# A hybrid decoder step on one core: three logit banks, probabilities in five tiles, and another order for marking and for the opening

## The chip, the cores and the metric

The kernel runs on one core of one Trainium2 chip. The metric is the time of one execution in microseconds (us) on the device, taken as the median of three runs. A profile of one execution (the trace) is read beside it. TensorE is PE in the profile and its weight loads are PEld; VectorE is DVE, ScalarE is ACT, GpSimd is POOL, and SyncE (SP) issues most of the DMA transfers.

## The reference, cut to what matters

One inference step of a decoder layer: a prompt of 1024 tokens and 8 sequences of 4 sampled tokens with 1024 cached keys each, width 1024, all in float32. The input is normalised and modulated by a condition, multiplied by one wide matrix, and split into an attention part, an indexer part, a retention part and gates.

```python
h, gate = modulated_input(x, c, w_ada, b_ada, g_norm)          # silu(c) @ w_ada: shift, scale, gate
qa, ka, va, za, qi, ki, wi, qr, kr, vr, zr, ga, gr = split_projection(h @ w_in)
s = sum_h relu(qi_h @ ki.T) * wi_h                             # index scores, 4 heads of 64
idx = top_k(where(key <= query, s, -inf), 256)                 # exact top 256, ties by lower index
y_a = softmax(qa @ k[idx] / 8) @ v[idx] * silu(za)             # 8 heads of 64
y_r = group_norm(retention(rotary(qr), rotary(kr), vr)) * g_ret * silu(zr)
merged = sigmoid(ga) * (y_a @ w_pa) + sigmoid(gr) * (y_r @ w_pr)
y = rms_norm(x + gate * (merged @ w_out), g_final)
```

It also returns the new keys, values, indexer keys and retention states.

## The kernel before, in words

Precision comes from splitting: a float32 operand becomes a rounded high part and a low rest, and a product is three matmuls (high by high, high by low, low by high). Rounding is a copy on ScalarE, the rest a subtraction on VectorE or GpSimd. The stages, by the profile's time:

1. **Opening (0 to 63 us).** `x_load` fetches the tokens, `x_block` turns them, `norms` finds their scales. For each of eight slices k of the width, `load_wa(k)` fetches two blocks of 512 KB of `w_ada`, `modulation(k)` multiplies them by the conditions (L212), turns the sums (L328) and reduces them to `cm`; `h_tile(k)` makes the modulated input `HH[k]` and its rest `HL[k]` (ScalarE L348, VectorE L349). `start_two(W)` (L235) begins the first two projections as the slices appear; its weights `ws` are loaded after `load_wa(0)`, rounded at L395 and L398 and their rests taken at L400. `idle_products` are matmuls of zeros, which fill PE.
2. **Projections, index scores, search, retention (63 to 545 us).** `project_parts` runs the projections (L218 to L220) from the list `order`. In their shadow VectorE and ScalarE search the 256th largest score of every query bit by bit (`pick_all`, `count`, `count_signs`); `exact` and `finish` then mark the keys that are not picked. `finish(j)` counts (L870), compares for equality on GpSimd (L922), numbers the equal ones by a scan (L923), combines (L924, L925) and writes the mask `BI[b]` in bf16 on ScalarE (L926). Its index j is 0 to 4 for blocks 6 to 2, 5 (`NP - 2`) for block 7, and 6 (`NP - 1`) for the sampled tokens. `retention` works pair by pair of heads; `gate_rows` makes a part of the output gate by products (L212), a copy (L523), a sum over partitions (L525) and a store.
3. **Cached keys and values (545 to 810 us).** Projections go on while GpSimd gathers cache pages (L1061, with the row numbers `idx` from L1051) for the sampled tokens.
4. **Prompt attention (810 to 967 us).** Sixteen steps (four pairs of heads, each in four pairs of query blocks that make nine key blocks together). `logits` multiplies (L1214, L1215) into a bank `lg`, VectorE adds the mask and takes the maximum (L1216), ScalarE the exponential, GpSimd the scale (L1223). `turn` transposes the probabilities by PE into a bank `tr` (L1236) and copies them to the tile `PT` (L1238); `combine` multiplies them by the values into a bank `po` (L1253, 36 products), and every second step VectorE reads `po` out (L1259). Logits run two steps ahead. `side` is the retention part's output projection (L1024 to L1026), in pieces of 12 matmuls, put between the steps.
5. **Output (967 to 1115 us).** The attention's and the final projection, the norm, the stores.

PSUM has eight banks in the attention: `lg` 2, `tr` 2, `po` 2, and `pj` 2 for the projections.

Each engine executes its own queue in order. The order of each queue is written before the run by a planner, which simulates the program with its own costs and takes the instruction that it finds ready, by priority (the order of the source). `issue_after(x)` makes the instructions inside it follow x on x's engine. Tiles are handed out by name from pools with a number of buffers: a writer waits until the readers of the buffer's last content are done.

Of the kernel before, what the change touches and what calls it, by code (L numbers as in the profile page):

```python
# [8 lines left out]
F32 = mybir.dt.float32  # L9
F32R = mybir.dt.float32r  # L10
BF = mybir.dt.bfloat16
# [106 lines left out]
def _hybrid_step(ctx, tc, A, outs, dbg):  # L118
# [122 lines left out]
    with ExitStack() as s0:  # L241
# [92 lines left out]
        def h_tile(k, pm):  # L334

            shift = BB[:, k, 0:1]
            nc.scalar.activation(AA[:, k], pm[:, 9:18], AF.Identity, bias=cg[:, k:k + 1], scale=cols[:, 24 + k:25 + k])
            nc.scalar.activation(shift, pm[:, 0:1], AF.Identity, bias=cols[:, k:k + 1])
            h = XT[:, k]
            nc.vector.scalar_tensor_tensor(h[:, :T], h[:, :T], AA[:, k, 0:1], RB[:, :T], op0=OP.mult, op1=OP.mult)  # L340
# [28 lines left out]
        W, ws = [], []  # L369
        zeros = sp.tile([128, 640], BF, name="zeros")  # L370
        nc.vector.memset(zeros, 0.0)

        def idle_products(n, behind):

            x = pl()
            with tc.issue_after(behind):
                for i in range(n):
                    nc.tensor.matmul(x[:, 512 * (i % 2):512 * (i % 2) + 512], zeros[:, :128], zeros[:, 128:], start=True, stop=True)

        for k in range(KT):  # L380
            load_wa(k)
            if k == 0:
                with tc.issue_after(loads[-1].ins):
                    ws = [wload(wp, w_in, f, 128) for f in (O_KI, O_QI)]
                pm, turned = modulation(k)
                idle_products(8, turned)
            else:
                with tc.issue_after(spread):
                    pm, turned = modulation(k)
            head_ends = h_tile(k, pm)  # L390
            if k == 0:
                for i in (0, 1):
                    wh, wl = [sp.tile([128, KT, 128], F32R, name="w", bufs=4) for _ in "hl"]
                    if i == 0:
                        nc.scalar.copy(wh, ws[i])  # L395
                    else:
                        with tc.issue_after(head_ends[0].ins):
                            nc.scalar.copy(wh, ws[i])  # L398
                    with tc.issue_after(head_ends[1].ins):
                        nc.vector.tensor_sub(wl, ws[i], f32(wh))  # L400
                    W.append((wh, wl))
        first = start_two(W)
# [95 lines left out]
    def retention(gp):  # L498
        with ExitStack() as s3:
            rp = s3.enter_context(tc.tile_pool(name="rp", bufs=1, reuse_waits="tile"))  # L500
            RC = rp.tile([128, R_ALL], F32, name="rc")
            nc.sync.dma_start(RC, A["rcs"])
            O = rp.tile([128, 9, 2, 64], F32, name="O")
            nc.gpsimd.memset(O[:, 8], 0.0)
            SD = rp.tile([128, 8, 128], F32, name="SD")
            nc.gpsimd.memset(SD, 0.0)
            for p in range(4):
                rows = split_rows(gp, O_QA + 128 * p, p, q_rows, qs)
                pair(rp, RC, O, SD, p, rows)
                for _ in rows:  # L510
                    pass
                gates(gp, (4 + 2 * p,))
                gate_rows(rp, p)
                gates(gp, (5 + 2 * p,))

    def gate_rows(rp, p):

        x = pj()
        for o in (0, 1):
            w = wload(wp, A["w_ada"][0], 2 * D + 256 * p + 128 * o, 128)  # L520
            ada_rows(x[:, 128 * o:128 * o + 128], lambda k: w[:, k])
        parts_, sums = [rp.tile([128, CH], F32, name="zt", bufs=2)[:, :256] for _ in (0, 1)]
        nc.scalar.copy(parts_, x[:, :256])  # L523
        x = pj()
        nc.tensor.matmul(x[:32, :256], C[:, C_SEL:C_SEL + 32], parts_, start=True, stop=True)  # L525
        nc.scalar.copy(sums[:9], x[:9, :256])
        nc.scalar.dma_start(GD[:, 256 * p:256 * p + 256], sums[:9])

# [186 lines left out]


    k_out, v_out, ki_out, st_out, ks_out, vs_out, kis_out, sts_out = outs[2:]

    with ExitStack() as s1:
# [4 lines left out]
        with ExitStack() as s2:  # L724
# [74 lines left out]
            gidx = selp.tile([128, NB], I32, name="gidx")  # L799
            gio = ip.tile([128, NB], I32, name="gio")  # L800
# [113 lines left out]
        def finish(j):  # L914
# [6 lines left out]
            t = thr[:n, j:j + 1]  # L921
            nc.gpsimd.tensor_scalar(eq[:n, :W], sc, t, 1.0, op0=OP.is_equal, op1=OP.mult)  # L922
            nc.vector.tensor_tensor_scan(ra[:n, :W], eq[:n, :W], eq[:n, :W], 0.0, op0=OP.add, op1=OP.bypass)  # L923
            nc.vector.scalar_tensor_tensor(ra[:n, :W], ra[:n, :W], rem[:n, j:j + 1], eq[:n, :W], op0=OP.is_gt, op1=OP.mult)  # L924
            nc.vector.scalar_tensor_tensor(ra[:n, :W], sc, t, ra[:n, :W], op0=OP.is_lt, op1=OP.add)  # L925
            nc.scalar.activation(bi, ra[:n, :W], AF.Copy, scale=MASKNEG)  # L926

# [8 lines left out]
        def pick_all():  # L936
# [100 lines left out]

    QU = 2
    NQ = 8 // QU
    sv = ctx.enter_context(tc.tile_pool(name="sv", bufs=1, reuse_waits="tile"))  # L1040
# [7 lines left out]
    by_pair = lambda d: d[:, T:].rearrange("(h p) c -> p h c", p=128)  # L1048
    idx = sv.tile([128, NQ, NB], I32, name="idx")
    for u in range(NQ):  # L1050
        nc.vector.tensor_scalar(idx[:, u], gidx, float(NQ), float(u), op0=OP.mult, op1=OP.add)  # L1051
    ks, zs, YS = [sv.tile([128, 4, NS], F32, name=n) for n in ("ks", "zs", "ys")]
# [147 lines left out]
    def logits(ap, step):  # L1200
# [4 lines left out]
        for b in blocks:  # L1205
            W = (b + 1) * 128
            for i, (k, qh, ql) in enumerate(ops):
# [3 lines left out]
                for n0 in range(0, W, 512):  # L1211
                    n1 = min(W, n0 + 512)
                    x = pbank("lg", 2)
                    nc.tensor.matmul(x[:, :n1 - n0], qh[:, qb], k[:, n0:n1], start=True, stop=False)  # L1214
                    nc.tensor.matmul(x[:, :n1 - n0], ql[:, qb], k[:, n0:n1], start=False, stop=True)  # L1215
# [12 lines left out]
    def turn(ap, step):  # L1228

        lg = step["lg"]  # L1230
        PT = step["PT"] = ap.tile([128, 18, 128], F32, name="pT", bufs=1)
        for j0 in range(0, 18, 4):
# [4 lines left out]
            flip[0] += 1  # L1237
            (nc.vector.tensor_copy if flip[0] % 3 == 0 else nc.scalar.copy)(PT[:, j0:j0 + m].rearrange("p j c -> p (j c)"), x[:, :128 * m])  # L1238

    def combine(ap, step):  # L1240
# [3 lines left out]
        if step["half"] == 0:  # L1244
            step["po"][0] = pbank("po", 2)
        po = step["po"][0]

        slot = {b: i for i, b in enumerate(sorted(step["group"]))}
        run = [(b1, kb, b0 + 1 + kb) for kb in range(b1, -1, -1)] + [(b0, kb, kb) for kb in range(b0, -1, -1)]

        def product(b, kb, j, i):
            r = slice(64 * i, 64 * i + 64)
            return nc.tensor.matmul(po[r, 128 * slot[b]:128 * slot[b] + 128], V[:, kb, r], PT[:, 2 * j + i], start=(kb == b), stop=(kb == 0))  # L1253
        step["last"] = together([lambda b=b, kb=kb, j=j, i=i: product(b, kb, j, i) for b, kb, j in run for i in (1, 0)])
# [10 lines left out]
    with ExitStack() as s4:  # L1265
# [238 lines left out]
```

## Time and profile before

| what | value |
|---|---|
| median of three runs | 1117.72 us (1115.03 to 1120.34) |
| profiled execution, its own time | 1117.12 us |
| its span | 1115.3 us, 20512 instructions |
| busy, of the span | PE 97%, PEld 89%, DVE 61%, ACT 43%, POOL 23% |
| mean granted TensorE clock | 0.993 |
| DMA | 185.63 MB, 166 GB/s |

The list of waits tells for each engine which instruction stood still and who released it; the timeline lists the instructions with the idle time before them in brackets; a row of windows gives busy time by engine in a stretch. Matmul ends are modelled, so a PE that is shown busy can still wait a little.

### The profile page before, as it was taken

The page shows a single profiled execution, that of the slowest core. Times are in us where ns is not written, and L with a number is a line of the kernel's source. Part 1 is how long each engine was busy: PE and PEld are TensorE (multiplying, and loading weights), DVE is VectorE, ACT ScalarE, POOL GpSimd, SP SyncE. Part 2 cuts the span into 40 slices and gives each one's busy share as a digit, 9 for nine tenths or more (in the row PEclk, how much of TensorE's full clock was granted, in tenths as well). Part 3 has the DMA queues.
Part 4 walks back from the last instruction along what each step waited for, and adds up shares of the span by engine and source line. Part 5 has one row for each costly group of instructions (what it writes and reads, how often), then busy time and mean ns, then how long its engine had stood idle before and what let it go on. Part 6 is the DMA issues. An engine that isn't in the chain of part 4 may idle for free. (4 is left out here: it accounts for less than half of the span.)

```text
span 1115.3 us, 20512 instructions
## 1 busy us (share of the span) xinstructions
PE 1085.7 (97%) x8137; PEld 987.9 (89%) x8138; DVE 680.3 (61%) x1632; ACT 478.0 (43%) x923; POOL 253.4 (23%) x202
## 2 busy tenths in 40 slices
PE   7999999999999999989999999999999999999997
PEld 6889899899989989989999998887988888898776
DVE  6776349698877868888422222210356777497765
ACT  6574445554654455333343333311335666443211
POOL 0003006113311220263242222244113333100000
PEclk9999999999999999999999999999999999999999
DMA  9923335265244515523787757386797520367431
GB/s 308 243 72 105 112 101 151 54 203 140 82 149 126 164 46 181 155 61 92 256 286 232 234 183 247 112 286 240 243 310 273 182 99 30 111 202 257 152 122 58
DMA packets 156024, 185.63 MB, mean 166 GB/s; under 512 B 18630, under 2 KB 126990, under 8 KB 154839
## 3 DMA queue, kind: packets, MB, share of 16 engines
q1 hardware_dynamic: 145632, 147.80, 42.5%
q0 software_dynamic: 9856, 35.66, 9.5%
q8 instruction: 64, 1.05, 0.4%
q10 hardware_dynamic: 438, 0.86, 0.2%
q14 instruction: 34, 0.27, 0.1%
HBM read 139.33 MB, written 41.17 MB: 162 GB/s over the span
## 5 line engine op out<-in xcount | busy, mean ns | idle before, releaser
L218 PE MATMUL pj<-hh,wh 128*128 128x352 f32 (+1 forms) x1168 | 383.4, 328 | 0.3 <-DVE qs L747 0.3
L219 PE MATMUL pj<-hl,wh 128*128 128x352 f32 (+1 forms) x1168 | 379.6, 325 | 0.0
L220 PE MATMUL pj<-hh,wl 128*128 128x352 f32 (+1 forms) x1168 | 378.6, 324 | 0.0
L218 PEld LDWEIGHTS pj<-hh,wh 128*128 128x128 f32 x1168 | 219.8, 188 | 8.2 <-issue 6.7
L219 PEld LDWEIGHTS pj<-hl,wh 128*128 128x128 f32 x1168 | 220.5, 189 | 5.1 <-issue 4.6
L220 PEld LDWEIGHTS pj<-hh,wl 128*128 128x128 f32 x1168 | 219.9, 188 | 4.4 <-issue 4.0
L870 DVE TENSOR_SCALAR_CACHE_REDUCE eq<-sc,cand 128x896 bf16<-128x896 f32 (+4 forms) x155 | 135.7, 876 | 2.6
L204 ACT CAST wh<-ws 128x1024 fp32r<-128x1024 f32 (+1 forms) x65 | 61.0, 942 | 115.4 <-PE pj L219 79.1
L205 POOL TENSOR_TENSOR wl<-ws,wh 128x1024 fp32r<-128x1024 f32 x18 | 45.1, 2506 | 147.0 <-ACT wh L204 146.9
L1223 POOL TENSOR_SCALAR lg<-lg,st 128x1024 f32<-128x1024 f32 (+7 forms) x64 | 48.0, 759 | 122.9 <-DVE st L1222 110.6
L205 DVE TENSOR_TENSOR wl<-ws,wh 128x1024 fp32r<-128x1024 f32 (+1 forms) x47 | 53.3, 1136 | 27.6 <-ACT wh L204 25.6
L1221 ACT ACTIVATE lg<-lg,st 128x1024 f32<-128x1024 f32 (+7 forms) x64 | 49.5, 775 | 25.0 <-DVE st L1220 23.3
L1094 DVE COPY kt<-str 128x512 f32<-128x512 f32 x32 | 22.1, 690 | 55.3 <-PE str L1092 48.0
L1061 POOL DMA_INDIRECT kv<-in_cache_k,idx x32 | 30.1, 941 | 94.2 <-PE str L1092 79.5
L1415 PE MATMUL pj<-woh,MH 128*128 128x512 f32 (+1 forms) x136 | 51.4, 378 | 0.0
L1416 PE MATMUL pj<-wol,MH 128*128 128x512 f32 (+1 forms) x136 | 51.2, 377 | 0.0
L1417 PE MATMUL pj<-woh,ML 128*128 128x512 f32 (+1 forms) x136 | 51.2, 377 | 0.0
L713 ACT ACTIVATE raw<-pj 128x352 f32<-128x352 f32 x48 | 22.1, 462 | 54.1 <-PE pj L220 48.4
L1236 PE MATMUL tr<-C,lg 128*128 128x128 f32 x288 | 43.6, 276 | 1.6 <-POOL lg L1223 0.5
L1061 POOL DMA_INDIRECT kv<-in_cache_v,idx x32 | 30.6, 957 | 52.8 <-PE sx L1122 27.8
L1236 PEld LDWEIGHTS tr<-C,lg 128*128 128x128 f32 x288 | 33.3, 140 | 9.5 <-issue 2.4
L1094 ACT COPY kt<-str 128x512 f32<-128x512 f32 x32 | 18.8, 589 | 50.0 <-PE str L1092 50.0
(352 smaller groups left out, 2002.1 us busy)
## 6 DMA issues: line engine op xcount, KB each, us to landing
ws<-in_w_in SPq DMA_DIRECT2D x51, 512.0 KB
rot<-in_rot SPq DMA_DIRECT2D x8, 1056.0 KB
x<-in_w_ada SPq DMA_DIRECT2D x16, 512.0 KB
TG<-raw SPq DMA_DIRECT2D x15, 528.0 KB
wst<-in_w_out SPq DMA_DIRECT2D x12, 512.0 KB
u<-TG SPq DMA_DIRECT2D x8, 528.0 KB
t<-TG SPq DMA_DIRECT2D x8, 528.0 KB
x<-in_x_prompt SPq DMA_DIRECT2D x8, 512.0 KB
```

Of the source, the lines that this page charges most:

```text
L204: nc.scalar.copy(wh[:, :, :n], ws[:, :, :n])
L205: (nc.vector if k == 4 or len(order) % 3 else nc.gpsimd).tensor_sub(wl[:, :, :n], ws[:, :, :n], f32(wh[:, :, :n]))
L218: nc.tensor.matmul(p, wh[:, k], HH[k][:, sl], start=(k == 0), stop=False)
L219: nc.tensor.matmul(p, wh[:, k], HL[k][:, sl], start=False, stop=False)
L220: nc.tensor.matmul(p, wl[:, k], HH[k][:, sl], start=False, stop=(k == KT - 1))
L870: nc.vector.tensor_scalar(junk[:n, :W], sc, thr[:n, j:j + 1], 0.0, op0=op, op1=OP.add, accum_out=cnt[:n, j:j + 1])
L1061: nc.gpsimd.indirect_dma_start(out=t.rearrange("p s c -> p (s c)"), out_offset=None, in_=cache.rearrange("g (r s) h d -> (g r) (s h d)", s ...
L1221: nc.scalar.activation(l, l, AF.Exp, bias=st[:, 2:3], scale=0.125, accum_out=st[:, 3:4])
L1236: step["turned"] = nc.tensor.transpose(x[:, 128 * (j - j0):128 * (j - j0) + 128], lg[:, j % 2, 128 * (j // 2):128 * (j // 2) + 128], ident)
L1415: nc.tensor.matmul(x, MH[:, k, tk], wh[:, k], start=(k == 0), stop=False)
L1416: nc.tensor.matmul(x, MH[:, k, tk], wl[:, k], start=False, stop=False)
L1417: nc.tensor.matmul(x, ML[:, k, tk], wh[:, k], start=False, stop=(k == KT - 1))
```

## The change

Six edits in one:

- **Opening.** `load_wa(k + 1)` is issued one slice ahead, so the second slice's weights stand ahead of `ws` in SP's queue. The first rounding of `ws` now follows the `moved` activation of slice 0 (it was free), the second stays behind `high` of slice 0; the rests follow `scaled` and `rest` of slice 1 instead of `rest` of slice 0. The tile of zeros shrinks.
- **gate_rows.** The sum over partitions and its store come after the next gate's projection.
- **idx.** The row numbers are computed in stage 2, behind the first whole score row.
- **finish.** The equality and the final scaling move to VectorE.
- **Order of marks.** Blocks 7 and 6 behind the third pair's norm, blocks 5 to 2 behind the fourth pair's masked scores; no further tie to projections.
- **Attention.** `lg` has three banks and `po` one; `PT` becomes five tiles with five buffers; the first block's values are added in rising order of keys; three of the nine first side pieces follow the first logits.

```diff
-            return high, rest
+            return high, rest, moved, scaled
...
+        load_wa(0)
         for k in range(KT):
-            load_wa(k)
+            if k + 1 < KT:
+                load_wa(k + 1)
...
-            head_ends = h_tile(k, pm)
+            ends.append(h_tile(k, pm))
             if k == 0:
                 for i in (0, 1):
...
+                    with tc.issue_after(ends[0][0 if i else 2].ins):
+                        rounded(i)
+            if k == 1:
+                for i in (0, 1):
+                    with tc.issue_after(ends[1][1 if i else 3].ins):
+                        rest(i)
...
-                gate_rows(rp, p)
+                summed = gate_rows(rp, p)
                 gates(gp, (5 + 2 * p,))
+                summed()
...
+                for u in range(NQ):
+                    nc.vector.tensor_scalar(idx[:, u], gidx, float(NQ), float(u), op0=OP.mult, op1=OP.add)
...
-            nc.gpsimd.tensor_scalar(eq[:n, :W], sc, t, 1.0, op0=OP.is_equal, op1=OP.mult)
+            nc.vector.tensor_scalar(eq[:n, :W], sc, t, None, op0=OP.is_equal)
...
-            nc.scalar.activation(bi, ra[:n, :W], AF.Copy, scale=MASKNEG)
+            nc.vector.tensor_scalar(bi, ra[:n, :W], MASKNEG, None, op0=OP.mult)
...
-            with tc.issue_after(normed[2].ins):
-                for j in (NP - 2, NV - 1, NV - 2):
-                    finish(j)
-            for i, j in enumerate(range(NV - 3, -1, -1)):
-                with tc.issue_after(masked[3].ins), tc.issue_after(marks[73 + i][0]):
-                    finish(j)
+            for behind_, js in ((normed[2], (NP - 2, 0)), (masked[3], range(1, NV))):
+                with tc.issue_after(behind_.ins):
+                    for j in js:
+                        finish(j)
...
-                    x = pbank("lg", 2)
+                    x = pbank("lg", 3)
...
-        PT = step["PT"] = ap.tile([128, 18, 128], F32, name="pT", bufs=1)
+        PT = step["PT"] = []
...
+            PT.append(ap.tile([128, 512], F32, name="pT", bufs=5))
...
-            step["po"][0] = pbank("po", 2)
+            step["po"][0] = pbank("po", 1)
...
-        run = [(b1, kb, b0 + 1 + kb) for kb in range(b1, -1, -1)] + [(b0, kb, kb) for kb in range(b0, -1, -1)]
+        run = [(b1, kb, b0 + 1 + kb) for kb in range(b1, -1, -1)] + [(b0, kb, kb) for kb in range(b0 + 1)]
...
-        for _ in zip(range(9), side):
+        for _ in zip(range(6), side):
             pass
+        for i in (0, 0, 1):
+            with tc.issue_after(steps[i]["begun"]):
+                next(side)
```

More of the change, by code (lines that the diff above doesn't have):

```diff
@@ L369, in _hybrid_step @@
         W, ws = [], []
-        zeros = sp.tile([128, 640], BF, name="zeros")
+        zeros = sp.tile([128, 512], BF, name="zeros")
         nc.vector.memset(zeros, 0.0)
@@ L377, in idle_products @@
                 for i in range(n):
-                    nc.tensor.matmul(x[:, 512 * (i % 2):512 * (i % 2) + 512], zeros[:, :128], zeros[:, 128:], start=True, stop=True)
+                    nc.tensor.matmul(x[:, 512 * (i % 2):512 * (i % 2) + 512], zeros[:, :128], zeros, start=True, stop=True)
+        W = [[sp.tile([128, KT, 128], F32R, name="w", bufs=4) for _ in "hl"] for _ in (0, 1)]
+        rounded, rest = lambda i: nc.scalar.copy(W[i][0], ws[i]), lambda i: nc.vector.tensor_sub(W[i][1], ws[i], f32(W[i][0]))
+        ends = []
+        load_wa(0)
         for k in range(KT):
-            load_wa(k)
+            if k + 1 < KT:
+                load_wa(k + 1)
             if k == 0:
@@ L389, in _hybrid_step @@
                     pm, turned = modulation(k)
-            head_ends = h_tile(k, pm)
+            ends.append(h_tile(k, pm))
             if k == 0:
                 for i in (0, 1):
[L393 to L401, printed above, removed]
+                    with tc.issue_after(ends[0][0 if i else 2].ins):
[4 more added lines that the diff above has]
+                        rest(i)
+        head_ends = ends[-1]
         first = start_two(W)
@@ L523, in gate_rows, with summed @@
         nc.scalar.copy(parts_, x[:, :256])
[L524 to L527, printed above, removed]
+        def summed():
+            x = pj()
+            nc.tensor.matmul(x[:32, :256], C[:, C_SEL:C_SEL + 32], parts_, start=True, stop=True)
+            nc.scalar.copy(sums[:9], x[:9, :256])
+            nc.scalar.dma_start(GD[:, 256 * p:256 * p + 256], sums[:9])
+        return summed
     def big(rp, name):
@@ L714, in gates @@
             (nc.scalar if j == 15 else nc.sync).dma_start(TG[128 * j:128 * j + 128], t)
+    QU = 2
+    NQ = 8 // QU
     k_out, v_out, ki_out, st_out, ks_out, vs_out, kis_out, sts_out = outs[2:]
@@ L799, in _hybrid_step @@
             gidx = selp.tile([128, NB], I32, name="gidx")
+            idx = selp.tile([128, NQ, NB], I32, name="idx")
             gio = ip.tile([128, NB], I32, name="gio")
@@ L1048, in _hybrid_step @@
     by_pair = lambda d: d[:, T:].rearrange("(h p) c -> p h c", p=128)
-    idx = sv.tile([128, NQ, NB], I32, name="idx")
-    for u in range(NQ):
-        nc.vector.tensor_scalar(idx[:, u], gidx, float(NQ), float(u), op0=OP.mult, op1=OP.add)
     ks, zs, YS = [sv.tile([128, 4, NS], F32, name=n) for n in ("ks", "zs", "ys")]
@@ L1212, in logits @@
                     n1 = min(W, n0 + 512)
-                    x = pbank("lg", 2)
-                    nc.tensor.matmul(x[:, :n1 - n0], qh[:, qb], k[:, n0:n1], start=True, stop=False)
+                    x = pbank("lg", 3)
+                    begun = nc.tensor.matmul(x[:, :n1 - n0], qh[:, qb], k[:, n0:n1], start=True, stop=False)
+                    step.setdefault("begun", begun.ins)
                     nc.tensor.matmul(x[:, :n1 - n0], ql[:, qb], k[:, n0:n1], start=False, stop=True)
@@ L1237, in turn @@
             flip[0] += 1
-            (nc.vector.tensor_copy if flip[0] % 3 == 0 else nc.scalar.copy)(PT[:, j0:j0 + m].rearrange("p j c -> p (j c)"), x[:, :128 * m])
+            PT.append(ap.tile([128, 512], F32, name="pT", bufs=5))
+            step["copied"] = (nc.vector.tensor_copy if flip[0] % 3 == 0 else nc.scalar.copy)(PT[-1][:, :128 * m], x[:, :128 * m])
     def combine(ap, step):
@@ L1244, in combine @@
         if step["half"] == 0:
-            step["po"][0] = pbank("po", 2)
+            step["po"][0] = pbank("po", 1)
         po = step["po"][0]
         slot = {b: i for i, b in enumerate(sorted(step["group"]))}
-        run = [(b1, kb, b0 + 1 + kb) for kb in range(b1, -1, -1)] + [(b0, kb, kb) for kb in range(b0, -1, -1)]
+        run = [(b1, kb, b0 + 1 + kb) for kb in range(b1, -1, -1)] + [(b0, kb, kb) for kb in range(b0 + 1)]
         def product(b, kb, j, i):
             r = slice(64 * i, 64 * i + 64)
-            return nc.tensor.matmul(po[r, 128 * slot[b]:128 * slot[b] + 128], V[:, kb, r], PT[:, 2 * j + i], start=(kb == b), stop=(kb == 0))
+            return nc.tensor.matmul(po[r, 128 * slot[b]:128 * slot[b] + 128], V[:, kb, r], PT[j // 2][:, 256 * (j % 2) + 128 * i:256 * (j % 2) + 128 * i + 128],
+                                    start=(kb == (b if b == b1 else 0)), stop=(kb == (0 if b == b1 else b)))
         step["last"] = together([lambda b=b, kb=kb, j=j, i=i: product(b, kb, j, i) for b, kb, j in run for i in (1, 0)])
```

6 lines of the change are left out of this document (2 added, 4 removed).

## The prediction, on record before the run

> **What bounds the kernel now.** I read the page's first part, then PE's list of waits over the whole span, then windows of stages, then timelines of the engine that each wait names.
>
> ```profile
> span 1115.3 us, 20512 instructions
> PE 1085.7 (97%) x8137; PEld 987.9 (89%) x8138; DVE 680.3 (61%) x1632; ACT 478.0 (43%) x923; POOL 253.4 (23%) x202
> PE pl L291 <- DMA x<-in_x_sample: 4.4, 1, 4.4
> PE pt L212 <- DMA x<-in_w_ada: 2.6, 3, 1.1
> PE pt L543 <- ACT vtok L584: 1.9, 1, 1.9
> PE pl L782 <- DVE qs L747: 1.4, 1, 1.4
> PE pb L621 <- DVE tmp L627: 1.3, 2, 1.1
> PE lg L1214 <- DVE st L1216: 1.0, 4, 0.3
> PE pj L525 <- ACT zt L523: 0.9, 1, 0.9
> PE tr L1236 <- DVE pT L1238: 0.3, 1, 0.3
> PE tr L1236 <- ACT pT L1238: 0.3, 1, 0.3
> ...
> 36.00:63.00 27.00, 26.19 (x250) 23.91 (x251) 19.28 (x40) 15.38 (x32) 1.66 (x1) 0.96 0.64 164
> 472.00:504.00 32.00, 28.93 (x245) 27.45 (x244) 27.66 (x31) 10.84 (x21) 18.48 (x7) 0.95 0.29 79
> 829.00:965.00 136.00, 132.81 (x1180) 114.26 (x1179) 96.02 (x368) 83.80 (x192) 46.85 (x63) 1.00 0.41 144
> 1107.00:1116.00 9.00, 0.19 (x2) 0.00 (x0) 3.43 (x14) 1.18 (x3) 0.00 (x0) 0.66 0.16 59
> ```
>
> PE is busy for 1085.7 of 1115.3 us, so 29.6 us is all that its shown gaps hold (in the wait rows the numbers are total us, times, longest). 4.4 us of it is the first load and 8.8 us the tail after the last matmul; the change touches neither. Its places are the w_ada wait (2.6), the vtok and tmp waits of the marking stage (1.9 and 1.3), the sum over partitions (0.9) and the attention's lg and pT waits (1.0, 0.3, 0.3): 8.3 us together. The window rows give length, then busy us of PE, PEld, DVE, ACT and POOL: PE leads in each stage, so a gap that is closed anywhere moves everything behind it forward, transfers included, unless a load sets the pace there. No matmul of the kernel's result is added or removed; the change can only close or open gaps.
>
> **Opening.**
>
> ```profile
> 8.72 3.44 SPq L358 DMA_DIRECT2D x<-in_w_ada  x2
> 12.21 5.13 SPq L198 DMA_DIRECT2D ws<-in_w_in  x2
> 17.45 26.02 SPq L358 DMA_DIRECT2D x<-in_w_ada  x14
> 21.99 1.05 ACT L395 CAST w<-ws 128x1024 fp32r<-128x1024 f32 x1
> 26.02 0.64 PE L212 MATMUL pt<-x,scT 128*32 128x128 f32 x16 [0.49 <-DMA x<-in_w_ada]
> 27.71 0.64 PE L212 MATMUL pt<-x,scT 128*32 128x128 f32 x16 [1.06 <-DMA x<-in_w_ada]
> 28.29 0.59 PE L235 MATMUL pj<-hh,w 128*128 128x352 f32 x2
> 34.71 1.08 PE L212 MATMUL pt<-x,scT 128*32 128x128 f32 x16 [1.08 <-DMA x<-in_w_ada]
> ```
>
> SP issues 14 loads in 26.02 us, 1.86 us each: the queue moves at the pace of the transfers. Slice 1's two loads pass the two of `ws`, so they land some 3.7 us sooner and the waits of 0.49 and 1.06 at slice 1's products go. `ws` lands 3.7 us later: its rounding, at 21.99 before, ends by 21.99 + 3.7 + 1.05 = 26.7 at the latest, still ahead of the first product at 28.29. Slice 3's load (1.08 us) has the same bytes ahead of it and stays; it is what is late next. The two rests on DVE now stand behind slice 1's work rather than ahead of it. From 36 us on PE works 26.19 of 27 us, so what is gained before then is kept. Term: -1.6 us. Ends: 0, where PE's new order lets slice 2's products, whose loads come no sooner, stand ahead of products that are ready; -2.6, all three waits. A loss up to 1.6 is possible if the later rests hold up products, and is kept for the range. The smaller tile of zeros costs nothing: DVE writes it while PE waits for the first load.
>
> **gate_rows and idx.** The 0.9 us wait of L525 is one of four sums; the product followed its copy by too little. With a projection between, it is gone: -0.9. The product moves behind that projection on PE, its small copy and the store's issue behind the projection's copies on ScalarE; what is stored is read only in the output stage, and the buffers of the partial sums are next written by the following pair, so this costs 0. idx is four small instructions, 0.38 us, that leave the end of the marking and go to where DVE is less than half busy.
>
> ```profile
> 100.00:150.00 50.00, 50.00 (x320) 41.72 (x318) 19.35 (x36) 21.75 (x36) 5.50 (x6) 1.00 0.37 111
> 533.34 0.38 DVE L1051 TENSOR_SCALAR idx<-gidx 128x8 int32<-128x8 int32 x4
> 542.95 1.03 POOL L1061 DMA_INDIRECT kv<-in_cache_k,idx  x1 [0.16 <-issue]
> ```
>
> The first gather runs 9 us after idx exists, so idx doesn't set it: 0.
>
> **Marking.**
>
> ```profile
> 455.29 0.76 DVE L905 TENSOR_SCALAR eq<-sc,base 128x1024 f32<-128x1024 f32 x1
> 473.77 6.96 POOL L922 TENSOR_SCALAR eq<-sc,base 128x1024 f32<-128x1024 f32 x1 [9.14 <-DVE eq L870]
> 480.76 2.83 DVE L923 TENSOR_TENSOR_SCAN ra<-eq 128x1024 f32<-128x1024 f32 x1 [1.53 <-POOL eq L922]
> 483.63 3.22 DVE L924 SCALAR_TENSOR_TENSOR ra<-ra,rem,eq 128x1024 f32<-128x1024 f32 x1
> 486.88 1.28 DVE L925 SCALAR_TENSOR_TENSOR ra<-sc,base,ra 128x1024 f32<-128x1024 f32 x1
> 488.20 1.06 ACT L926 ACTIVATE bi<-ra 128x1024 bf16<-128x1024 f32 x1 [6.80 <-DVE ra L925]
> DVE ra L923 <- POOL eq L922: 5.2, 5, 1.6
> ```
>
> Here is a chain: GpSimd takes 6.96 us for one comparison, DVE waits for it, ScalarE stands 6.80 us at the mask of block 7 with the copies of the values queued behind, and PE waits 1.9 us for those (L543, above). With comparison and mask on DVE, ScalarE's queue no longer holds that instruction: -1.9. The prices on DVE: a comparison by L905 is 0.76 us for 1024 columns, seven of them have 5280 columns, 3.9 us; the mask (one tensor in, bf16 out) has no row, between the same 3.9 and 6.6 us by L925 (1.28 for 1024); I take 3.9, as L905 too has one tensor in. So 7.8 us are added to DVE, against 5.2 us of waits for GpSimd and 1.9 us by which L924 exceeds L925 at one size while GpSimd works beside it: nearly even. GpSimd loses the comparisons and is on no path here. The tmp wait (1.1 of its 1.3 us before the fourth pair's score products) is DVE behind schedule; the two blocks ahead of it now are the widest two (1920 columns, as 1024 + 384 + 512 before), so DVE is hardly earlier: -0.5, between -1.1 and +2.0 (one block's L923 or L924, up to 3.2 us, in front of L627, less the 1.1 that is waited already). The prompt's marks are read only by the attention, nearly 300 us after the marking (533 to 829 in the rows). Term: -2.4, between -3.0 and +0.1.
>
> **Attention.**
>
> ```profile
> PEld lg L1214 <- DVE st L1216: 4.3, 12, 0.5
> PEld tr L1236 <- ACT pT L1238: 2.0, 7, 0.5
> PEld tr L1236 <- DVE pT L1238: 0.8, 2, 0.5
> 856.47 2.19 PE L1253 MATMUL po<-pT,V 128*64 128x128 f32 x36
> 865.81 2.19 PE L1253 MATMUL po<-pT,V 128*64 128x128 f32 x36
> L1259 DVE TENSOR_TENSOR y<-po,za x7: 673/692/692, 849.5 to 952.5; 128x512 f32<-128x512 f32 x7
> ```
>
> The third bank addresses the wait of L1214 for L1216. PE shows 1.0 us of it, its loader 4.3, since a late load is partly covered by the matmul before it; the truth lies between. Taken: 1.8, nearer to PE's own row. Five tiles let the copies of the next step start before the last of 36 products; that addresses pT, 0.6 on PE, 2.8 on the loader: 0.7 taken. The first product still waits for the copy turned last, before and after, so its order there is worth nothing. The planner may also cut the step into longer runs; I count none of it. Side pieces behind the first logits only fill the same gaps: 0. One `po` bank adds a wait: the next group's first product, with the transposes and logits queued behind it on PE, for L1259. A step takes 9.34 us (856.47 to 865.81), 2.19 of it the products, so the cover is about 7.1 us for a read of 0.69: 0. Term: -2.5, between -7.1 (the loader's three rows) and 0.
>
> [...]
>
> **The sum.** Any edit of the order shifts the planner's choices elsewhere; waits it does not aim at (L782, 1.4 us, for one) can grow, and I allow +1.0 for one of about that size. -1.6 - 0.9 - 2.4 - 2.5 + 1.0 = -6.4. The profiled execution took 1117.12 us (span 1115.3 and 1.8 around it), which gives 1110.7; the median of the runs, 1117.72, stands 0.6 above, so I put the time at 1111.
>
> **The rivals.**
>
> *Only half arrives.* PE's queue is fixed beforehand by estimated durations; the opening stays tied to its loads (term 0), the tmp wait stays, and the attention gives only PE's own 1.6. Then -0.9 - 1.9 - 1.6 + 1.0 = -3.4, some 1114. For it: each PE wait in the attention is at most 0.3 us, and the loads of w_ada fill the queue to 43.5 us. Against: PE is packed after 36 us.
>
> *The single `po` bank costs more than all gains: slower.* If DVE's queue puts L1259 behind a step's mask work, the next group waits. DVE works 96.02 us in 136, 6.6 us per step of 9.34, so one step's work ahead of the read (7.3 us with it) about uses up the cover; it decides once the read ends 8.9 us or more after the products: 1.8 us by 7 groups is 12.6, and the net is +6.2, about 1124. Against: the first read starts at 849.5, at once after its products.
>
> *The loader's waits are the real ones.* The attention yields 7.1: -1.6 - 0.9 - 2.4 - 7.1 + 1.0 = -11.0, about 1106. For it: twelve waits of L1214's load, spread over the steps; against: PE was shown without work for only 1.0 of those 4.3 us.
>
> **How the numbers follow.** Forecast 0.42, half 0.34, loader 0.15, slower 0.09. The forecast's own range is 1109 to 1113. A measurement of this kernel tells about 0.5% (5.6 us) from no change: below 1112.1 is faster. Faster: loader 0.15 and most of the forecast, 0.33, with a little of the half case, 0.02: 0.50. Same: 0.41. Slower: 0.09. The range is 1104 to 1118: it takes in the loader case with two us of its own spread, the half case and an opening or tmp term that turns into a loss (+1.6 and +2.0 in place of -1.6 and -0.5 make -0.3, 1117), and leaves out the slow one and about 0.05 below.
>
> **What would show it.** Right: no wait of L212 for w_ada longer than 0.5 us until slice 3, the opening's last L235 some 1.6 us sooner; no L525 wait; no ACT wait of several us at the mask and none of PE for vtok; fewer PEld waits of L1214; DVE's reads of `po` within 7 us. Wrong: DVE's queue late at L627 or L597, ScalarE late at the rounding of `ws`, products waiting for the rests of slice 1, or L1253 waiting for L1259.

## The result and the profile after

Five executions of each kernel, taken together: the changed kernel has a median of 1106.62 us (1105.81 to 1107.04), the kernel before 1116.36 us (1115.03 to 1120.34). The ratio is 0.9904, with a 95% interval of 0.9888 to 0.9920: 9.7 us by the medians, faster by more than the 0.5% that can be told. The prediction was 1111 (1104 to 1118).

The profiled execution took 1106.86 us. Its first part, and the head of PE's list of waits (total us, times, longest), which answer to the first fence of the prediction:

```profile
span 1105.1 us, 20498 instructions
PE 1078.5 (98%) x8138; PEld 982.2 (89%) x8138; DVE 679.3 (61%) x1646; ACT 471.8 (43%) x916; POOL 229.5 (21%) x195
PE pl L291 <- DMA x<-in_x_sample: 4.1, 1, 4.1
PE pj L235 <- ACT hh L348: 2.3, 3, 1.6
PE pl L291 <- DVE xt L299: 2.2, 2, 1.4
PE pt L212 <- DMA x<-in_w_ada: 1.9, 3, 1.1
PE pl L791 <- DVE qs L756: 1.3, 1, 1.3
PE str L1097 <- ACT kt L1099: 0.9, 1, 0.9
PE pj L218 <- ACT raw L720: 0.8, 1, 0.8
...
PE tr L1242 <- ACT pT L1245: 0.6, 2, 0.3
PE lg L1219 <- DVE st L1222: 0.6, 2, 0.4
...
PE po L1260 <- ACT pT L1245: 0.5, 1, 0.5
PE tr L1242 <- DVE pT L1245: 0.5, 1, 0.5
```

The waits for vtok (1.9), for tmp (1.1 of it) and for zt (0.9) are gone. A new one stands at L218 (0.8), the opening's wait of L235 for `hh` grew from 0.8 to 2.3, and the attention's rows still hold 2.2 us. (Lines moved: L218 to L235, L291 and L348 kept their numbers, 525 is now 531, 621 is 628, 627 is 634, 922 to 926 are 934 to 938, 1214 is 1219, 1216 is 1222, 1238 is 1245, 1253 is 1260, 1259 is 1267.)

Windows of PE in the marking stage (length, then busy us of PE, PEld, DVE, ACT and POOL, then PEclk), the kernel before first:

```profile
488.00:492.00 4.00, 2.06 (x14) 1.53 (x13) 2.83 (x7) 2.73 (x5) 1.57 (x1) 1.00 0.25 76
492.00:496.00 4.00, 4.00 (x17) 4.00 (x16) 2.53 (x7) 1.83 (x5) 2.43 (x2) 0.57 0.00 0
```

and the changed kernel:

```profile
488.00:492.00 4.00, 4.00 (x64) 3.77 (x64) 3.33 (x3) 2.20 (x5) 1.82 (x2) 1.00 0.02 4
492.00:496.00 4.00, 4.00 (x65) 3.36 (x62) 4.00 (x8) 0.67 (x3) 0.00 (x0) 1.00 0.46 133
```

Behind the stall of 1.9 us the granted clock of the kernel before fell to half (0.57 over this window) for 3.41 us. PE is shown busy in that window all the same: no list of waits holds this loss.

**Where the time went.** A list of waits can't be summed into a gain, so I matched the n-th matmul of each kind in two traces and took how much later it starts, counted from the start of the span, as a median over the 20 us from each bound. The differences of that shift between stages, in us against the profile of the kernel before (negative is shorter):

| kernel | opening, to 80 | 80-460 | marking, 460-520 | 520-560 | 560-800 | attention, 800-980 | sum |
|---|---|---|---|---|---|---|---|
| **changed kernel** | -2.3 | -0.8 | -4.7 | +1.6 | -0.9 | -3.1 | -10.1 |
| marks_engines | -0.6 | +0.1 | -4.2 | +0.5 | -1.6 | +0.2 | -5.6 |
| marks_eq | -0.3 | +0.1 | -4.2 | +0.1 | +0.6 | 0.0 | -3.7 |
| marks_mask | +0.1 | -0.1 | +3.8 | -0.2 | -1.3 | +0.2 | +2.6 |
| marks_order | -0.5 | +0.1 | +5.4 | +0.6 | +0.5 | +0.1 | +6.1 |
| stall_filled | -0.9 | +0.1 | +1.8 | 0.0 | -1.7 | 0.0 | -0.7 |
| stall_filled3 | -0.7 | +0.1 | +1.8 | 0.0 | -0.2 | +0.2 | +1.2 |
| banks_only | -1.1 | 0.0 | +1.5 | 0.0 | +0.9 | +0.8 | +2.2 |
| tiles_only | -1.1 | +0.1 | +1.7 | 0.0 | -0.3 | -0.5 | 0.0 |
| after_no_open | -1.0 | -0.7 | -4.7 | +1.6 | -0.8 | -3.1 | -8.6 |
| after_no_side | -1.9 | -0.9 | -4.7 | +1.6 | -2.1 | -3.3 | -11.2 |
| after_last_sum | -1.8 | -0.7 | -4.7 | +0.4 | -1.3 | -3.1 | -11.2 |
| three_undone | -2.2 | -0.9 | -4.6 | +0.3 | -0.7 | -3.1 | -11.2 |

The rows repeat each other where the code is the same: that gives the scatter. In the opening and from 560 to 800 us equal code differs by 1 to 3 us from trace to trace. From 80 to 460 us and in the attention it agrees within 0.2.

### The profile page after: what moved, and what is told of

It reads as the page before. It is cut to its first block, busy times and chain, and to the rows that moved or that the text cites. A ratio compares the mean times of both kernels' runs of the same rounds, so it can differ in the third digit from the quotient of the medians.

```text
span 1105.1 us, 20498 instructions
## 1 busy us (share of the span) xinstructions
PE 1078.5 (98%) x8138; PEld 982.2 (89%) x8138; DVE 679.3 (61%) x1646; ACT 471.8 (43%) x916; POOL 229.5 (21%) x195
## 5 line engine op out<-in xcount | busy, mean ns | idle before, releaser
L218 PE MATMUL pj<-hh,wh 128*128 128x352 f32 (+1 forms) x1168 | 383.5, 328 | 1.0 <-ACT raw L720 0.8
L218 PEld LDWEIGHTS pj<-hh,wh 128*128 128x128 f32 x1168 | 219.3, 188 | 10.5 <-issue 7.5
L205 DVE TENSOR_TENSOR wl<-ws,wh 128x1024 fp32r<-128x1024 f32 (+1 forms) x47 | 52.6, 1122 | 35.7 <-ACT wh L204 35.4
L205 POOL TENSOR_TENSOR wl<-ws,wh 128x1024 fp32r<-128x1024 f32 x18 | 43.1, 2394 | 147.6 <-ACT wh L204 147.6
L720 ACT ACTIVATE raw<-pj 128x352 f32<-128x352 f32 x48 | 22.1, 463 | 53.0 <-PE pj L220 46.1
```

The lines of the kernel that those rows point to most:

```text
L205: (nc.vector if k == 4 or len(order) % 3 else nc.gpsimd).tensor_sub(wl[:, :, :n], ws[:, :, :n], f32(wh[:, :, :n]))
L218: nc.tensor.matmul(p, wh[:, k], HH[k][:, sl], start=(k == 0), stop=False)
```

## The experiments

The first theory was the prediction's, with one addition from the trace: ScalarE's scaling of a mark holds up the vtok copy, and the stall costs half a clock behind it as well. The rivals were the order of the marks, and the comparison on GpSimd.

**marks_engines**: both operations on VectorE, nothing else.

```diff
-            nc.gpsimd.tensor_scalar(eq[:n, :W], sc, t, 1.0, op0=OP.is_equal, op1=OP.mult)
+            nc.vector.tensor_scalar(eq[:n, :W], sc, t, None, op0=OP.is_equal)
...
-            nc.scalar.activation(bi, ra[:n, :W], AF.Copy, scale=MASKNEG)
+            nc.vector.tensor_scalar(bi, ra[:n, :W], MASKNEG, None, op0=OP.mult)
```

> The kernel before with one part of the change: both marking steps (the equality and the final scaling) on VectorE, the old order of marks kept. Theory (ScalarE's blocked queue, and the clock): the wait of 1.9 us for vtok goes, the one of 1.1 us for tmp goes too, and the stretch of half clock behind them (492.1 to 495.5 us, about 1.7 us) goes with the stall: about 4.5 us off 1116.4, 1112, and a granted clock of 1.00 from 480 to 540 us. Rival 1 (the order of marks made the gain): no change, 1116. Rival 2 (only the listed waits count, the clock costs nothing): 3.0 us off, 1113.4, with the half-clock stretch still there or gone at no price.

Measured: 1111.31 us against 1116.65, ratio 0.9953 (0.9939 to 0.9966). More than half of the whole gain comes from these two lines. The vtok wait and the tmp wait of this stage are gone (0.2 us of tmp is left, of an earlier pair); a wait of 0.6 us for `ss` is new.

**marks_order**: the new order alone.

```diff
-            with tc.issue_after(normed[2].ins):
-                for j in (NP - 2, NV - 1, NV - 2):
...
+            for behind_, js in ((normed[2], (NP - 2, 0)), (masked[3], range(1, NV))):
```

> The kernel before with only the new order of marks (blocks 7 and 6 behind the third pair's norm, 5 to 2 behind the fourth pair's masked scores), engines as before. Theory: ScalarE still scales the marks ahead of the vtok copy, so a wait of 1 to 2 us for vtok and a half-clock stretch stay: within 1 us of 1116.4. Rival (the order made the gain): 4 to 5 us off, 1112.

Measured: 1121.56 against 1116.65, ratio 1.0038 (1.0026 to 1.0049). Slower by more than the 1 us that the theory allowed. PE's waits from 300 to 545 us in this kernel:

```profile
PE pt L609 <- ACT kd L587: 3.7, 1, 3.7
PE pt L543 <- ACT vtok L584: 2.1, 1, 2.1
```

With 896 columns where 384 and 512 stood, ScalarE waits 6.62 us for the mark and holds the copies of kd as well; the granted clock is at half from 500.1 to 510.4 us. The order is no gain with the old engines.

**marks_mask**: only the scaling on VectorE (the second pair of lines above).

> The kernel before with only the final scaling of a mark (L926) moved from ScalarE to VectorE; the equality stays on GpSimd, the order stays. Theory: the vtok wait of 1.9 us goes and the half-clock stretch with it, the tmp wait of 1.1 us stays or grows by the 0.5 to 2.5 us of a scaling that now stands ahead of L627 on VectorE: 2.5 to 3.6 us off, about 1113. Rival (the equality on GpSimd was what held the chain up): the vtok wait stays at about 1.9 us, under 1 us off, 1116.

Measured: 1119.38 against 1116.65, ratio 1.0024 (1.0014 to 1.0034): slower. The vtok wait is gone, as the theory said, and a larger wait stands at tmp. PE's row, then VectorE's timeline (start, us, instruction, idle before it and its releaser), then a window of the stage:

```profile
PE pb L621 <- DVE tmp L627: 5.8, 2, 5.6
...
501.97 1.88 DVE L627 TENSOR_TENSOR tmp<-pb,dm 128x512 f32<-128x512 f32 x3
...
504.00:508.00 4.00, 4.00 (x20) 3.67 (x16) 2.50 (x5) 2.27 (x2) 1.48 (x1) 0.50 0.21 60
```

L627 begins at 501.97 us, against 501.32 in the kernel before:

```profile
501.32 1.88 DVE L627 TENSOR_TENSOR tmp<-pb,dm 128x512 f32<-128x512 f32 x3
```

VectorE's own chain is what is late, and freeing ScalarE only moved the place where PE meets it. The stage is 3.8 us longer although L627 is only 0.65 later: by the matched matmuls the shift is about +1 us at 502 us and +3.8 at 506. It grows behind the wait of 5.6 us, where PE is shown busy and the granted clock is at half (499.3 to 509.6 us).

**marks_eq**: only the comparison on VectorE (the first pair of lines); ScalarE still scales.

> The kernel before with only the equality (L922) moved from GpSimd to VectorE; ScalarE still does the final scaling, the order stays. Theory, formed on the three runs before this one (the equality's trip to GpSimd, 6.33 us for 1024 columns, makes the whole mark late, and ScalarE only waited for it): the mark of block 7 is ready some 7 us sooner, neither the vtok wait of 1.9 us nor the tmp wait of 1.1 us is left, and the kernel is 4 to 5 us faster, about 1112. Rival (as predicted: the scaling in ScalarE's queue holds the vtok copy): the vtok wait stays within 0.5 us of 1.9, and the gain is under 1.5 us, 1115 to 1116.5.

Measured: 1112.51 against 1117.09, ratio 0.9967 (0.9956 to 0.9978). In its list of PE's waits from 300 to 545 us neither vtok nor a tmp wait of size is left, although ScalarE still stands before a mark with the vtok copies behind it:

```profile
PE pj L525 <- ACT zt L523: 0.8, 1, 0.8
PE pb L621 <- DVE tmp L627: 0.2, 1, 0.2
...
481.19 1.06 ACT L926 ACTIVATE bi<-ra 128x1024 bf16<-128x1024 f32 x1
...
486.74 0.52 ACT L926 ACTIVATE bi<-ra 128x384 bf16<-128x384 f32 x1 [1.73 <-DVE ra L925]
...
496.16 1.88 DVE L627 TENSOR_TENSOR tmp<-pb,dm 128x512 f32<-128x512 f32 x3
```

The mark of block 7 is scaled at 481.19 us, 7.0 us sooner than before (488.20). So the comparison's trip to GpSimd is the cause, ScalarE's queue only the place where it showed. In the trace the two operations together give -4.2 in the marking stage, and so does the comparison alone. L627 then begins at 496.16 us, 5.2 us sooner than before. How much of that is the 6.96 us itself and how much the VectorE work that ran slower beside GpSimd (L923 and L924 for 1024 columns 2.83 and 3.22 us before, 2.29 and 1.28 here), no run separates.

**stall_filled**: does the half clock cost anything? Ten matmuls of constants ahead of the waiting transposition.

```diff
+                    if p == 3 and c == 1 and i == 0:
+                        fill = ps.tile([128, 512], F32, name="pb", bufs=3)
+                        for _ in range(10):
+                            nc.tensor.matmul(fill[:, :352], C[:, :128], C[:, :352], start=True, stop=True)
```

> The kernel before with ten matmuls of constants (128x352 each, result unused, 0.16 us from start to start) put ahead of the transposition that waits 1.9 us for vtok; no other instruction of PE moves. Theory (a stall of nearly 2 us makes the clock half for the next 3.41 us, which costs 1.7 us): PE stands still for the same time less the fillers' 1.6 us, its granted clock stays 1.00 from 488 to 500 us, and the kernel is 1.7 us faster although the transposition starts no sooner: about 1114.7. Rival (the stall alone costs, the clock nothing): no change or up to 0.3 us slower, 1116.4 to 1116.7.

Measured: 1117.75 against 1116.65, ratio 1.0009 (1.0000 to 1.0017). Inconclusive: the fillers were mis-costed, as PE's timeline shows, and filled past the stall's end (its clock stayed at 1.00, and its stage is 1.8 us longer all the same, as the shift shows already at 502 us); the planner also moved one scaling on ScalarE ahead of copies.

```profile
487.65 6.08 PE L606 MATMUL pb<-C 128*128 128x352 f32 x20
```

**stall_filled3**: three fillers, and the moved scaling tied to its old place.

```diff
-                        for _ in range(10):
+                        for _ in range(3):
...
+                with tc.issue_after(kd_copied[3].ins):
+                    nc.scalar.activation(bi, ra[:n, :W], AF.Copy, scale=MASKNEG)
```

> As stall_filled, with three fillers for ten (a filler took 0.59 us there, two passes, not the 0.16 us assumed) and with the 512-column scaling of a mark held at its old place in ScalarE's queue, which the ten fillers had moved; no other instruction of any engine moves. The fillers fit in the stall of 1.9 us. Theory (the stall makes the clock half in the next 3.41 us where it falls into one such window): the granted clock stays 1.00 around 490 to 500 us and, where the profile of before lost 1.7 us there, the stretch from 488 to 500 us is shorter by 1 to 1.7 us; over the runs the gain is less, since not every run of before needs to have the stall in one window: 1115 to 1116.4. Rival (the clock costs nothing): the stretch is as long as in before, 1116.6.

Measured: 1118.34 against 1117.09, ratio 1.0012 (1.0001 to 1.0024): no gain. The clock did stay at 1.00 from 488 to 500 us, yet the next wait grew by what was saved: its vtok wait is 0.6 us, and the one for tmp (its lines are four further down) is

```profile
PE pb L625 <- DVE tmp L631: 2.5, 1, 2.5
```

tiles_only (below) shows the same without any filler: its instructions in this stage are those of the kernel before, but there the stall didn't lower the clock. First PE's waits from 470 to 520 us in tiles_only, then its windows:

```profile
PE pb L621 <- DVE tmp L627: 2.7, 1, 2.7
PE pt L543 <- ACT vtok L584: 2.0, 1, 2.0
492.00:496.00 4.00, 4.00 (x57) 3.77 (x57) 2.56 (x5) 3.39 (x9) 3.29 (x3) 1.00 0.00 0
500.00:504.00 4.00, 2.80 (x22) 2.63 (x23) 4.00 (x8) 0.50 (x1) 0.00 (x0) 0.78 0.45 131
504.00:508.00 4.00, 4.00 (x23) 4.00 (x22) 0.99 (x4) 2.19 (x3) 2.42 (x1) 0.79 0.05 8
```

At full clock PE comes sooner to L621 and waits 2.7 us there for L627, where the kernel before showed 1.1: 2.0 + 2.7 against 1.9 + 1.7 + 1.1, the same 4.7 (1.7 is half of the 3.41 us at half clock). The half clock ahead of a wait cost nothing, since L627 set the end. So my addition (1.7 us for the clock at 492 us) falls. Behind the second stall, where PE next waits for nobody, a half-clock stretch (500 to 508 us here) does lengthen the stage: banks_only, tiles_only and stall_filled3, which have one there, are 1.5 to 1.8 us later than the profile of before, which had none there. By the matched matmuls their shift at 502 us is within 0.3 us of the one with which they entered the stage, and 1.5 to 1.8 us above it at 507. That is an inference from four traces; no run set the clock by itself.

**banks_only** and **tiles_only**: the two parts of the attention's change, each on the kernel before.

```diff
-                    x = pbank("lg", 2)
+                    x = pbank("lg", 3)
...
-            step["po"][0] = pbank("po", 2)
+            step["po"][0] = pbank("po", 1)
```

> The kernel before with one part of the attention's change: three banks for lg and one for po (one tile pT, old order of values and of side pieces). Theory (the third bank brings most of the 3.1 us that the stage from 810 to 970 us got shorter): the loader's wait of lg for VectorE's L1216 (4.3 us, 12 times in before) is gone and the stage is 1.8 to 2.5 us shorter, about 1114.5. Rival 1 (the five tiles bring it): 0 to 0.5 us, 1116.5. Rival 2 (one po bank costs): products wait for L1259, the stage is longer by 1 us or more.

```diff
-        PT = step["PT"] = ap.tile([128, 18, 128], F32, name="pT", bufs=1)
+        PT = step["PT"] = []
...
+            PT.append(ap.tile([128, 512], F32, name="pT", bufs=5))
...
-        run = [(b1, kb, b0 + 1 + kb) for kb in range(b1, -1, -1)] + [(b0, kb, kb) for kb in range(b0, -1, -1)]
+        run = [(b1, kb, b0 + 1 + kb) for kb in range(b1, -1, -1)] + [(b0, kb, kb) for kb in range(b0 + 1)]
```

> The kernel before with the other part of the attention's change: the turned probabilities in five tiles and the first block's values in rising order (two lg banks, two po banks, old side pieces). Theory (the third bank brings most): 0.5 to 1 us off the stage from 810 to 970 us, the loader's wait of lg for L1216 still at about 4 us, about 1116. Rival 1 (the five tiles bring it): 2 to 3 us off, 1114. Rival 3 (only both together bring it): 0 here and 0 with the banks alone, 1116.6 in both.

Measured: banks alone 1118.87 against 1117.09, ratio 1.0014 (1.0003 to 1.0025); tiles alone 1117.14, ratio 1.0000 (0.9991 to 1.0010). By stage: +0.8 and -0.5, where both together give -3.1. So neither theory nor rival 1 holds; rival 3 does. The loader's longest waits for another engine (PEld, 800 to 975 us) of banks_only, then of the changed kernel:

```profile
...
PEld tr L1236 <- ACT pT L1238: 3.5, 6, 1.2
PEld lg L1214 <- DVE st L1216: 2.6, 7, 0.5
PEld po L1253 <- ACT pT L1238: 1.4, 5, 0.4
PEld po L1253 <- DVE pT L1238: 1.4, 4, 0.8
```

```profile
...
PEld lg L1219 <- DVE st L1222: 2.1, 4, 0.6
PEld tr L1242 <- ACT pT L1245: 1.4, 3, 0.5
PEld po L1260 <- ACT pT L1245: 1.4, 4, 0.7
```

With the third bank and one tile pT, the wait for lg shrinks and the wait for the copies into pT grows instead: all the loader's rows for pT, of transposes and products, add up to 3.0 us before, 6.8 with the banks alone and 3.2 in the changed kernel. So the wait moves unless both are there. No row shows a wait for the single po bank.

**after_no_side**: the changed kernel with the nine side pieces together again.

```diff
-        for _ in zip(range(6), side):
+        for _ in zip(range(9), side):
             pass
-        for i in (0, 0, 1):
-            with tc.issue_after(steps[i]["begun"]):
-                next(side)
```

> The changed kernel (1106.6 us) with one edit of the attention undone: the nine first side pieces stand together ahead of the steps again, and none follows the first logits. Three lg banks, one po bank and five tiles stay. Theory (banks and tiles bring the 3.1 us only together, since the third bank alone made the stage 0.8 us longer and the tiles alone 0.5 us shorter): the stage from 810 to 970 us keeps at least 2.5 of the 3.1 us, 1107. Rival (the side pieces between the first logits bring it): the stage loses 2 us or more of it, 1109 to 1110.

Measured: 1106.08 us (1105.76 to 1106.80), ratio to before 0.9910 (0.9894 to 0.9925); its attention is 3.3 us shorter than before's. The side pieces' new places are worth nothing; banks and tiles are the pair that counts. No run has the pair alone on the kernel before.

**after_no_open**: the changed kernel with the old opening (`load_wa(k)` in its slice, the old places of the roundings and rests).

```diff
-            if k + 1 < KT:
-                load_wa(k + 1)
+            load_wa(k)
...
+                    with tc.issue_after(head_ends[1].ins):
+                        nc.vector.tensor_sub(wl, ws[i], f32(wh))
```

> The changed kernel with the opening undone (weights of w_ada one slice later in the queue, roundings and rests as before). Theory (the opening's edits are worth about 1.2 us; the other 0.85 us by which the profile of before was later there came with its two stretches of half clock, which the same opening doesn't show in another run): 1.0 to 1.5 us slower, 1107.8. Rival 1 (all of the 2.1 us is the edits'): 1108.7. Rival 2 (it is all the clock): 1106.6.

Measured: 1106.89 us (1106.28 to 1108.36), ratio to before 0.9914 (0.9900 to 0.9927). Against the changed kernel's 0.9904 the medians differ by about a microsecond at most, which these runs don't resolve. The traces say more: the ten with the old opening (the kernel before as 0) stand at +0.1 to -1.1 us at 80 us, mean -0.6; the four with the new one at -1.8 to -2.3, mean -2.1. The opening's edits are worth about 1.5 us. Neither group depends much on whether a half-clock stretch fell into it: in the new group the two that have one (after_no_side and after_last_sum, mean granted clock 0.996 and 0.997 against 0.998) stand some 0.4 us later than the two without.

**after_last_sum**: the changed kernel, the deferred sum kept for the first three pairs only.

```diff
+                if p == 3:
+                    summed()
                 gates(gp, (5 + 2 * p,))
-                summed()
+                if p < 3:
+                    summed()
```

> The changed kernel with the partition sum of gate_rows put after the next gate's projection for the first three pairs only; for the last pair it stands where it was. Theory (deferring the last pair's sum makes a product L218 wait 0.8 us for a copy L720 in ScalarE's queue, which takes back what the deferral won): that wait is gone and the stretch from 536 to 560 us is 0.5 to 0.9 us shorter; no wait of 0.8 us for zt comes in its place; about 1105.9. Rival 1 (the sum then waits 0.8 us for zt, as it did in before): 1106.6. Rival 2 (the wait for L720 has nothing to do with the sum): it stays, 1106.6.

Measured: 1105.48 us (1104.77 to 1105.79), every run under every one of the changed kernel (1105.81 to 1107.04); ratio to before 0.9900 (0.9885 to 0.9915). In the trace it is 1.1 us shorter from 520 to 560 us. From 500 to 600 us PE's waits are one row, where the changed kernel has L218's 0.8:

```profile
PE pt L713 <- POOL O L705: 0.3, 1, 0.3
```

The changed kernel's ScalarE at that place: the product L218 at 541.98 us waits 0.79 for L720, which stands behind a rounding.

```profile
540.52 1.04 ACT L204 CAST wh<-ws 128x1024 fp32r<-128x1024 f32 x1 [3.22 <-PE pj L219]
541.47 0.46 ACT L720 ACTIVATE raw<-pj 128x352 f32<-128x352 f32 x1
541.83 0.34 ACT L532 COPY zt<-pj 9x256 f32<-9x256 f32 x1
```

The rounding alone doesn't make the wait, since in after_last_sum the same copy stands behind one too (at 542.53 us) and PE waits for nothing there. That the deferral brings the wait is shown; by which link is not.

**three_undone**: the old order of marks (the lines of marks_order turned back), the last sum and the side pieces back, all in the changed kernel.

> The changed kernel with three of its edits undone, each in a stage of its own, so that the trace shows each by the stretch it lies in: the old order of marks (470 to 530 us), the last pair's sum where it was (536 to 560 us), the nine first side pieces together again (810 to 970 us). Theory (the new order of marks is worth nothing once the equality is on VectorE; the sum's return gains 1.1 us and the side pieces' 0.0 to 0.2, as each did alone): no new wait of PE from 470 to 530 us and that stretch within 0.3 us of the changed kernel's, the median 1105.3. Rival (the new order is worth 0.5 us or more, which a wait of 0.6 us for ss in the run with both operations moved and the old order hints at): the marking stretch is 0.5 to 1.0 us longer, the median 1106.

Measured: 1105.59 us (1105.30 to 1105.88), ratio to before 0.9898 (0.9882 to 0.9915). The marking stage is as in the changed kernel (-4.6 against -4.7). So the new order of marks is worth nothing once the comparison is on VectorE. This kernel and after_last_sum have the lowest medians here, about 1 us under the changed kernel. By the ratios, whose intervals overlap, the runs alone don't resolve that; the traces put it at 1.1 to 1.3 us from 520 to 560 us.

## Why the prediction was right, and where it was not

The direction held, and the time lies in the range, 4 us below the point: beyond the forecast's own 1109 to 1113. It came out at the time of the rival in which the loader's waits are the real ones (about 1106), but not by that mechanism: the attention gave 3.1 us, not 7.1. The range reached down there for that rival's sake, so that the time lies within it is in part luck. Of the 4 us, 1.4 is the base: the five runs put the kernel before at 1116.36, and the forecast started from 1117.72. Most of the rest is the marking. One sum of the range was also wrong: with +1.6 and +2.0 in place of -1.6 and -0.5 the terms make -0.7, not -0.3 (1117 either way).

- **Opening, -1.6: right in size** (about -1.5 over the traces). The waits of slice 1 went and slice 3's stayed (1.07 us), as written. A wait of 1.63 us for ScalarE's L348 came in their place. It is the sign of being wrong that I had named, ScalarE late at the rounding of `ws`: the rounding waits 1.75 us for its load, and L348 stands behind it. I had checked that the rounding ends before the first product's old time (26.34 us, against 28.29), but not what stands behind it in the queue.

```profile
25.30 1.04 ACT L381 CAST w<-ws 128x1024 fp32r<-128x1024 f32 x1 [1.75 <-DMA ws<-in_w_in]
26.25 1.36 ACT L348 ACTIVATE hh<-xt,BB 128x528 fp32r<-128x528 f32 x2
```

The listed waits of the opening are not smaller than with the old one, so by which of them the 1.5 us was won is not settled.
- **gate_rows, -0.9: right at its place, given back.** From 80 to 460 us it brought 0.8, all of it between 330 and 350 us, where the wait for zt was. The same deferral in the last pair made L218 wait, +1.1. The allowance of +1.0 for waits that the edits don't aim at was for just this, but I had named L782 for it and costed the move of the sum behind ScalarE's work at nothing. `idx` and the smaller tile of zeros were tested by no run of their own.
- **Marking, -2.4: the step that failed**, by 2.3 us against this profile (-4.7); two other profiles of this code in the kernel before, banks_only and tiles_only, are 1.5 and 1.7 longer here, so it may be 6 us. The vtok wait was put down to ScalarE's queue, because ScalarE stood 6.80 us at the mask. marks_mask and marks_eq show that it stood there for VectorE, and VectorE for GpSimd. And the tmp wait was costed at 1.1 us at the most: I took the two waits as two stalls, but they are one lateness of VectorE's chain, met twice, and the half clock between them hid 1.7 us of it. The row with PEclk 0.95 was in the first fence and no step used it. The argument that the widest blocks stand ahead now, so that L627 would be hardly earlier, was wrong: L627 begins at 501.32 us before and, as L634, here, 8.9 us sooner, of which 3.1 were won ahead of this stage.

```profile
492.46 1.88 DVE L634 TENSOR_TENSOR tmp<-pb,dm 128x512 f32<-128x512 f32 x3
```

The balance of VectorE's prices came out nearly even, but by two errors: the seven scalings took 8.1 us, not 3.9 (two of them, beside GpSimd, 2.50 and 2.23), and the scans and L924 became 5.8 us shorter, not 1.9. It was drawn over all seven marks, too, while only what stands ahead of L627 can hold it up.
- **Attention, -2.5: nearly right (-3.1), the split wrong.** 1.8 for the bank and 0.7 for the tiles are +0.8 and -0.5 alone. PE's own listed waits in the stage hardly changed (2.3 us before, with those for GpSimd and L1222; 2.2 after), so these rows did not measure what was won; the loader's wait for L1216 (now L1222) went from 4.3 us in 12 times to 2.1 in 4. The 7.1 of the loader's rival is the sum of the loader's waits; the stage gave 3.1: more than PE's rows (1.6), less than half of the loader's.
- **The single po bank: right.** No product waited for L1267, which began within 0.2 us of its products' end each time; the next group's products came 3.9 us or more after it began.
- **560 to 800 us** scatters from -2.1 to +0.9 in traces with no edit that counts there; the changed kernel's -0.9 is not put down to anything.

## What to carry to other kernels

When an engine stands long at an instruction, follow its releaser to the end of the chain before costing a move: here ScalarE waited for VectorE, which waited for GpSimd, and only the last link was worth moving. Two waits of the same chain are one lateness, and the second one's listed size is only what the work between left over; look at the granted clock between them. Test two halves of a buffering change alone and together: a bank without the tile behind it moved the wait and cost 0.8 us, both took 3.1 off.

## What the runs showed of the hardware

**The clock.** In the trace of the kernel before, the granted clock, recorded from 10.84 us on, is 1.00 but for three stretches of 3.41 us at 0.50 (from 14.25, 34.73 and 492.12 us) and the tail from 1109.93 us; from each of these starts to the next it is 6, 134 and 181 times 3.413 us. In the changed kernel only the tail is at 0.50, from 1101.01 us. In the kernel before the window from 488.7 to 492.1 us, shown 46% busy with one stall of 1.9 us, was followed by one at 0.50, and so were the 3.41 us from 10.84 and from 31.32 us, shown 66% and 51% busy; those from 24.49, 79.10 and 498.94 us, shown 55%, 59% and 67% busy, were followed by 1.00. The busy share alone doesn't tell the two groups apart. In tiles_only the clock was 1.00 behind the stall of 2.0 us (the windows from 484 to 488 and from 488 to 492 us, shown 90% and 58% busy), and 0.78 and 0.79 in the two windows from 500 to 508 us, behind the stall of 2.7 us.

**A comparison on GpSimd.** 1024 columns took 6.96 us there, beside work of VectorE, and 0.73 us on VectorE (the changed kernel's first row below); 640 columns, with little of VectorE beside them, 2.42 and 0.54 us. Some of VectorE's own work took longer beside GpSimd too: L924 took 3.22 us beside GpSimd's L205, and as L936 1.28 us without it; the new scaling of 1024 columns took 2.50 us beside L205. Rows of the changed kernel, then GpSimd's of the kernel before:

```profile
469.75 0.73 DVE L934 TENSOR_SCALAR eq<-sc,base 128x1024 f32<-128x1024 f32 x1
475.04 1.28 DVE L936 SCALAR_TENSOR_TENSOR ra<-ra,rem,eq 128x1024 f32<-128x1024 f32 x1
479.23 2.37 POOL L205 TENSOR_TENSOR wl<-ws,wh 128x1024 fp32r<-128x1024 f32 x1
479.66 2.50 DVE L938 TENSOR_SCALAR bi<-ra 128x1024 bf16<-128x1024 f32 x1
```

```profile
481.38 4.38 POOL L205 TENSOR_TENSOR wl<-ws,wh 128x1024 fp32r<-128x1024 f32 x1
...
563.44 2.39 POOL L205 TENSOR_TENSOR wl<-ws,wh 128x1024 fp32r<-128x1024 f32 x1
```

Beside L924 and the scan, L205 itself took 4.38 us, against 2.39 where no instruction of VectorE ran beside it. Beside the scaling VectorE alone was slow: L205 took 2.37 us. In marks_engines the same scaling began 0.12 us ahead of L205 and took 0.70 us, and the comparison of 384 columns began within L205 and took 2.48 us (0.41 in the changed kernel):

```profile
482.01 0.70 DVE L926 TENSOR_SCALAR bi<-ra 128x1024 bf16<-128x1024 f32 x1
482.13 2.82 POOL L205 TENSOR_TENSOR wl<-ws,wh 128x1024 fp32r<-128x1024 f32 x1
482.70 2.48 DVE L922 TENSOR_SCALAR eq<-sc,base 128x384 f32<-128x384 f32 x1
```

These are single meetings of two instructions; no run measured by itself what the two cost each other.
